# Layer 0's attention: one query ring for all head groups, a ring for weights alone with loads a unit sooner, late casts behind an exponential, modulation columns in another bank

## The chip, the cores and the metric

The kernel runs on one core of a Trainium2 chip. A core has five engines that each work through a queue of their own in order: PE (matrix products, into the accumulation memory PSUM), DVE and POOL (element-wise work), ACT (functions, copies and casts) and SP, which here only issues loads and stores. They meet through semaphores. The metric is the device time of one execution in microseconds (us).

## The reference, cut to what matters

Two layers of a backbone over 512 latent tokens and 256 context tokens of width 1024. Layer 0 mixes its tokens by two kinds of grouped attention, layer 1 by differential attention; each layer ends in a gated feed-forward block. The change touches only the mixer of layer 0 and, in it, the modulation vectors that are computed alongside:

```python
mx = (s_c @ mod_w[l] + mod_b[l])[:, None, :]          # modulation, six parts of 1024
hx = _rms(x, norm_mix_w[l]) * (1.0 + scx1) + shx1
qa, ka, va, qb, kb, vb = jnp.split(hx @ w_in, cuts, axis=-1)
qa, ka = _rope(_rms(qa, qn_a)), _rope(_rms(ka, kn_a))  # and the same for qb, kb
s = einsum(q, k) * scale; p = _softmax(s, sink)        # A: window of 128 and context; B: all tokens
out = einsum(p, v)                                     # then concatenated, @ w_out
```

There are 16 query heads of width 64. Four of them share a key and a value head; such a set of four is called a head group here. Groups 0 and 1 are of kind A, groups 2 and 3 of kind B. Products are made in single precision out of a rounded high part and a low part: a weight `wi` is cast on ACT to `wih` (the high part), and the rest `wil = wir - wih` is formed on DVE or POOL, so three products stand for one.

## The kernel before

**Tiles and steps.** The tokens are six tiles of 128 (four latent, two context). `in_proj0` projects one head group tile by tile: 24 products of 128x384 into one PSUM bank (`inps`), a copy to `qkv` on ACT (L529), norm and rotation on DVE and POOL, casts to `qd` and `kd`, and then two closures, `turn_q` and `turn_k`, which transpose the queries (`qpt`) and keys (`kpt`) on PE and copy them back on ACT (`qt`, L546, and `kT`, L553). `attend0` is a generator for one group and one tile: scores (`sc`), their maximum on DVE, the exponential on ACT (L601), the division on POOL (L613), transposes of the result (`ppt`, copied back by ACT at L626 and by DVE at L624) and the product with the values (`av`, copied by ACT at L634). The main loop takes 24 steps (b, t): in step (b, t) it attends group b, tile t, and puts the projection of one tile of group b+1 between the pieces.

**Order.** From the sixth step on PE's order is the order of the code (`manual_schedule`). Before that, and on all other engines throughout, the scheduler of the language sets the order when the program is built, by its own estimate of times.

**Weights.** A group needs four units of 256 rows of `ev_w_in`. `weights0` loads a unit with three DMAs into a staging tile `wir`, casts it on ACT (L507) and subtracts on DVE or POOL in turn (L508). The high and low parts go to rings of six tiles (`WBUF + 1`). Units 0 and 1 of group b+2 are made at step (b, 4), units 2 and 3 at the start of step (b+1, 0). The staging tiles come from `raw_tile`, a ring of two buffers (tag `raw`) that the modulation weights `modw` and the rotation table `rp` use as well.

**Modulation.** `mod_steps` computes 256 columns of one part: two loads of `modw`, 16 small products into the bank `acc0`, a copy `modr` (ACT, L185), and then, one step later, four products that turn the row into columns (`modcol`, L191), which DVE adds to `modc` (L279). `modcol` also stands in `acc0`, the bank of the projection's `inps`.

**Transposing banks.** `qpt`, `kpt` and `ppt` share two PSUM banks in turn (`tr0`, `tr1`); a transpose waits until the copy of what stood there before is done.

**Query tiles.** `qt` is a ring of six in a pool of the group's own: `odd` and `even` take turns, so there are two rings.

## Time and profile before

| what | value |
|---|---|
| median of 3 runs | 1686.17 us (1681.69 to 1688.62) |
| profiled execution | 1690.29 us, its span 1688.5 us |
| PE busy | 1629.1 us, 96% of the span |
| DVE, ACT, POOL busy | 1141.8, 935.7, 712.9 us |
| layer 0's attention with its projections | about 41 to 345 us of the span |

The span is the time from the first to the last instruction of the profiled execution; the rest up to its own time lies around it. In the rows below a time is a start in us from the span's beginning. A row of the timeline gives start, duration, engine, line of the code, operation, output and inputs, and, where the engine stood idle just before, how long and what ended it. In the rows of waits the numbers are the sum in us, how many, and the longest. `x4` at a row's end means that four instructions of one kind are merged in it.

### The profile page before, as it was taken

What the parts mean: (1) busy time and instruction counts of PE and PEld (TensorE: products, weight loads), DVE (VectorE), ACT (ScalarE), POOL (GpSimd) and SP (SyncE); (2) the same over time, 40 slices, a digit from 0 to 9 for tenths busy, and PEclk for the clock granted to TensorE, in tenths of its full rate; (3) what the DMA queues carried; (4) which work ended last, traced back from release to release, by engine and by line L of the source; (5) the groups of instructions that cost most, each with busy time, mean ns of one, the idle gap of its engine ahead of it and who ended that gap; (6) DMA issues with size and microseconds to landing.
All of it is one profiled execution on the core that took longest, in us unless ns stands there. A gap on an engine that the chain in (4) does not pass through costs nothing. (4 is left out here: it accounts for less than half of the span.)

```text
span 1688.5 us, 28522 instructions
## 1 busy us (share of the span) xinstructions
PE 1629.1 (96%) x10376; PEld 1466.7 (87%) x10376; DVE 1141.8 (68%) x1980; ACT 935.7 (55%) x2008; POOL 712.9 (42%) x872
## 2 busy tenths in 40 slices
PE   6999999899999999999999999999999999999998
PEld 3967787677999999998878799999987899999887
DVE  4765656554799988767767556666666598887433
ACT  5565555745456655545554456666666555555320
POOL 2665555621346554412413367776765342221000
PEclk8999999999999999999999999999999999999999
DMA  9222221411355555439866221111113333331431
GB/s 321 70 72 68 77 70 51 163 62 38 120 177 172 166 158 163 135 110 343 294 181 198 87 59 38 48 47 46 47 51 94 119 95 108 106 103 56 138 100 63
DMA packets 221693, 194.67 MB, mean 115 GB/s; under 512 B 20017, under 2 KB 206961, under 8 KB 221553
## 3 DMA queue, kind: packets, MB, share of 16 engines
q1 hardware_dynamic: 221200, 192.65, 37.1%
q8 instruction: 81, 1.33, 0.3%
q14 instruction: 60, 0.48, 0.1%
q10 hardware_dynamic: 352, 0.21, 0.0%
HBM read 179.94 MB, written 12.87 MB: 114 GB/s over the span
## 5 line engine op out<-in xcount | busy, mean ns | idle before, releaser
L928 ACT CAST wbh<-wr 128x512 fp32r<-128x512 f32 x170 | 104.8, 621 | 123.1 <-PE p L960 67.7
L960 PE MATMUL p<-hT,wbh 128*128 128x256 f32 (+1 forms) x752 | 154.0, 298 | 0.0
L474 PE MATMUL inps<-wih,hT 128*128 128x384 f32 x512 | 143.9, 343 | 2.6 <-ACT qkv L688 1.8
L938 POOL TENSOR_TENSOR wbl<-wr,wbh 128x512 fp32r<-128x512 f32 x43 | 58.5, 1360 | 173.5 <-ACT wbh L928 173.5
L960 PEld LDWEIGHTS p<-hT,wbh 128*128 128x128 f32 x752 | 122.1, 191 | 0.2
L938 DVE TENSOR_TENSOR wbl<-wr,wbh 128x512 fp32r<-128x512 f32 x127 | 107.1, 854 | 19.0 <-ACT wbh L928 14.9
L960 PE MATMUL p<-hT,wbl 128*128 128x256 f32 (+1 forms) x376 | 111.7, 297 | 0.0
L960 PE MATMUL p<-t,wbh 128*128 128x384 f32 (+1 forms) x480 | 110.8, 317 | 0.0
L613 POOL TENSOR_SCALAR Pt<-Pt,rc 128x256 f32<-128x256 f32 (+3 forms) x96 | 76.6, 810 | 67.0 <-DVE rc L610 58.2
L231 POOL TENSOR_TENSOR modp<-modp 128x512 f32<-128x512 f32 x40 | 56.5, 1412 | 113.5 <-ACT modp L230 113.5
L914 POOL TENSOR_TENSOR wr<-wr 128x512 f32<-128x512 f32 x40 | 62.3, 1558 | 92.5 <-DVE ws L919 92.5
L960 PE MATMUL p<-hTt,wbh 128*128 128x256 f32 (+1 forms) x480 | 100.8, 302 | 0.0
L474 PEld LDWEIGHTS inps<-wih,hT 128*128 128x128 f32 x512 | 93.4, 188 | 5.5 <-ACT qkv L688 2.8
L928 ACT CAST wbh<-ws 128x512 fp32r<-128x512 f32 x120 | 69.5, 580 | 44.4 <-PE p L960 29.7
L960 PE MATMUL p<-b,wbh 128*128 128x384 f32 x368 | 93.6, 335 | 0.5 <-DVE c L988 0.4
L224 DVE SCALAR_TENSOR_TENSOR ma<-modw,cols,ma 128x256 f32<-128x256 f32 x140 | 91.2, 651 | 2.5 <-DMA modw<-in_mod_w_dram 0.2
L601 ACT ACTIVATE Pt<-sc,nm 128x256 f32<-128x256 f32 (+3 forms) x96 | 67.8, 709 | 35.3 <-DVE nm L597 17.0
L474 PE MATMUL inps<-wil,hT 128*128 128x384 f32 x256 | 85.8, 335 | 0.0
L938 DVE TENSOR_TENSOR wbl<-ws,wbh 128x512 fp32r<-128x512 f32 x120 | 81.6, 680 | 1.7 <-ACT wbh L928 1.6
L960 PEld LDWEIGHTS p<-t,wbh 128*128 128x128 f32 x480 | 82.8, 189 | 0.0
L960 PEld LDWEIGHTS p<-hTt,wbh 128*128 128x128 f32 x480 | 78.4, 191 | 3.0 <-ACT modp L230 1.6
L474 PE MATMUL inps<-wihi,hT 128*128 128x384 f32 x256 | 75.7, 351 | 2.1 <-DVE modc L279 1.9
(359 smaller groups left out, 5214.0 us busy)
## 6 DMA issues: line engine op xcount, KB each, us to landing
modw<-in_mod_w_dram SPq DMA_DIRECT2D x96, 512.0 KB, 4.7
wr<-in_ffn_w_in_dram SPq DMA_DIRECT2D x176, 256.0 KB, 3.0
wdr<-in_ffn_w_out_dram SPq DMA_DIRECT2D x66, 512.0 KB, 3.7
wir<-in_od_w_in_dram SPq DMA_DIRECT2D x96, 128.0 KB, 2.3
hidm<-hid SPq DMA_DIRECT2D x44, 192.0 KB, 2.0
hr<-hidm SPq DMA_DIRECT2D x22, 192.0 KB, 3.5
x<-in_x_dram SPq DMA_DIRECT2D x8, 512.0 KB, 3.6
wir<-in_ev_w_in_dram SPq DMA_DIRECT2D x16, 256.0 KB, 3.6
```

Of the source, the lines that this page charges most:

```text
L224: nc.vector.scalar_tensor_tensor(acc, w[:, k], scale[k], acc, ALU.mult, ALU.add)
L231: nc.gpsimd.tensor_add(pr[:, 0:2], pr[:, 0:2], pr[:, 2:4])
L474: nc.tensor.matmul(ps, hs[j][:, k, :], ws[k // 2][z][:, k % 2, c0:c1], start=(k, j, z) == (0, 0, 0), stop=(k, j, z) == (KT - 1, 1, 0))
L601: turn["exp"] = nc.scalar.activation(p[:, :n], s, AF.Exp, bias=nm[:, c1], accum_out=sm[:, c1])
L613: nc.gpsimd.tensor_scalar(p[:, :n], p[:, :n], rc[:, hh:hh + 1], 1.0, ALU.mult, ALU.mult)
L914: nc.gpsimd.tensor_sub(w, raw[f, "G1"], w)
L928: nc.scalar.copy(hi, w)
L938: (nc.gpsimd if name == "G2" else nc.vector).tensor_sub(lo, raw[need[n]], f32(hi))
L960: nc.tensor.matmul(ps, w[:, k, :], H[b][h][:, k, :], start=first and k == 0 and q == 0, stop=final and k == 3 and q == 2, skip_group_check ...
```

## The change

There are six edits.

- `qt` is allocated in the pool of the whole attention (`at`), not in the group's own, so there is one ring of six for all groups.
- Staging tiles for the weights of groups 1 to 3 come from a ring of their own, two buffers with the tag `wir`; `raw` is left to `modw` and `rp`.
- In `weights0` the loads of unit 2 are issued when unit 1 is made and those of unit 3 with unit 2 (`loads`).
- The first loads of group 1 are put behind the load of `sink`.
- Units 2 and 3 of groups 2 and 3 are made after the first two pieces of step (b, 0), behind an exponential, and no longer ahead of that step.
- `modcol` in the attention stands in the bank `acc1`, that of `av`, and no longer in `acc0`.

```diff
-    def mod_steps(l, part, n, new_tile, pool, bank, wide=None, room=("modr", 1)):
+    def mod_steps(l, part, n, new_tile, pool, bank, wide=None, room=("modr", 1), cols_bank=None):
...
-        pc2 = p_1.tile([P, nb, 2], F32, name="modcol", tag=bank)
+        pc2 = p_1.tile([P, nb, 2], F32, name="modcol", tag=cols_bank or bank)
...
-    def weights0(b, wp, subs, new_tile=raw_tile, loads=((0, 1), (), (2,), (3,))):
+    def weights0(b, wp, subs, new_tile=raw_tile, loads=((0, 1), (2,), (3,), ())):
...
-                qt = st.tile([P, 4, P], F32R, name="qt", tag="qt", bufs=6)
+                qt = at.pool.tile([P, 4, P], F32R, name="qt", tag="qt", bufs=6)
...
-    nc.sync.dma_start(sink, dram_rows(ev_sink_a[0]))
+    turn["sink"] = nc.sync.dma_start(sink, dram_rows(ev_sink_a[0]))
...
-                mod_runs.append(mod_steps(*mods.pop(0), raw_tile, at.pool, "acc0"))
+                mod_runs.append(mod_steps(*mods.pop(0), raw_tile, at.pool, "acc0", cols_bank="acc1"))
...
-    units = weights0(1, wp.pool, (nc.gpsimd, nc.vector))
-    next(units)
+    def own_raw(shape, name):
+        return wp.pool.tile(shape, F32, name=name, tag="wir", bufs=2)
+
+    units = weights0(1, wp.pool, (nc.gpsimd, nc.vector), own_raw)
+    with behind("sink"):
+        next(units)
...
-                ws += units
+                if not b:
+                    ws += units
...
-                units = weights0(b + 2, wp.pool, (nc.gpsimd, nc.vector))
+                units = weights0(b + 2, wp.pool, (nc.gpsimd, nc.vector), own_raw)
...
                 transposes0(i - 1)
                 scores0(i)
+                if j == 0:
+                    with behind("exp"):
+                        ws += units
                 projected(n[0])
```

What the scheduler makes of it shows in the order of the instructions. On ACT, at the end of group 0's projection, just ahead of the first attention step, before:

```order
L449 ACTIVATE sq<-qkv 128x320 x2
L546 CAST qt<-qpt 128x512
L534 CAST qd<-qy 128x4x64
L553 CAST kT<-kpt 128x2x128
L538 CAST kd<-qy 128x128
L529 COPY qkv<-inps 128x384
L546 CAST qt<-qpt 128x512
```

and now:

```order
L449 ACTIVATE sq<-qkv 128x320
L507 CAST wihi<-wir 128x768 x2
L449 ACTIVATE sq<-qkv 128x320
L553 CAST kT<-kpt 128x2x128
L534 CAST qd<-qy 128x4x64
L538 CAST kd<-qy 128x128
L529 COPY qkv<-inps 128x384
L546 CAST qt<-qpt 128x512
```

The two casts are units 0 and 1 of group 2. They stood in the fourth step and now stand ahead of a key copy (`kT`) of group 0's last tiles.

On ACT, from the first attention step of group 1 into the next one, before:

```order
L626 COPY Pt<-ppt 128x4x128
L507 CAST wihi<-wir 128x768
L601 ACTIVATE Pt,sm<-sc,nm 128x256
L546 CAST qt<-qpt 128x512
L607 ACTIVATE es<-es 128x2
L507 CAST wihi<-wir 128x768
L626 COPY Pt<-ppt 128x4x128
L553 CAST kT<-kpt 128x2x128
L529 COPY qkv<-inps 128x384
```

and now:

```order
L546 CAST qt<-qpt 128x512
L601 ACTIVATE Pt,sm<-sc,nm 128x256
L507 CAST wihi<-wir 128x768 x2
L607 ACTIVATE es<-es 128x2
L626 COPY Pt<-ppt 128x4x128
L601 ACTIVATE Pt,sm<-sc,nm 128x256 x2
L607 ACTIVATE es<-es 128x2
L553 CAST kT<-kpt 128x2x128
L529 COPY qkv<-inps 128x384
L507 CAST wihi<-wir 128x768
L449 ACTIVATE sq<-qkv 128x320
L507 CAST wihi<-wir 128x768
```

The first pair of casts (units 2 and 3 of group 2) has moved behind the copy of the queries and an exponential. The second pair is units 0 and 1 of group 3, which stood four steps later; the copies of the step's values and transposes follow it.

On SP, the queue of the loads, the same part of the program, before:

```order
L177 DMA modw<-in_mod_w_dram 128x4x256 x2
L500 DMA wir<-in_ev_w_in_dram 128x2x256
L500 DMA wir<-in_ev_w_in_dram 128x2x64 x2
L500 DMA wir<-in_ev_w_in_dram 128x2x256
L500 DMA wir<-in_ev_w_in_dram 128x2x64 x2
L392 DMA rp<-in_rope_dram 128x512
L177 DMA modw<-in_mod_w_dram 128x4x256 x6
```

and now:

```order
L177 DMA modw<-in_mod_w_dram 128x4x256 x2
L392 DMA rp<-in_rope_dram 128x512
L177 DMA modw<-in_mod_w_dram 128x4x256 x2
L500 DMA wir<-in_ev_w_in_dram 128x2x256
L500 DMA wir<-in_ev_w_in_dram 128x2x64 x2
L500 DMA wir<-in_ev_w_in_dram 128x2x256
L500 DMA wir<-in_ev_w_in_dram 128x2x64 x2
```

Before, these loads of `wir` are units 2 and 3 of group 2; now those have been issued much earlier, and the ones shown are units 0 and 1 of group 3, ahead of which stands the table `rp`.

## Rows read from the trace of the kernel before

**Rows 1.** The page, busy time, share and instructions of PE:

```profile
PE 1629.1 (96%) x10376; PEld 1466.7 (87%) x10376; DVE 1141.8 (68%) x1980; ACT 935.7 (55%) x2008; POOL 712.9 (42%) x872
```

**Rows 2.** Windows: length, busy time of PE, PEld, DVE, ACT, POOL, PE's clock, DMA:

```profile
76.00:131.00 55.00, 49.87 (x363) 39.55 (x363) 35.63 (x109) 35.51 (x103) 37.06 (x64) 1.00 0.19 55
145.00:219.00 74.00, 68.85 (x521) 57.54 (x523) 47.31 (x127) 43.67 (x121) 39.83 (x66) 0.98 0.27 81
```

**Rows 3.** Waits of PE from 60 to 345 us:

```profile
PE ppt L621 <- ACT qt L546: 5.7, 5, 2.9
...
PE inps L474 <- DVE modc L279: 1.9, 3, 1.0
```

**Rows 4.** Timeline of PE, the stalls and one row without any:

```profile
74.38 0.55 PE L544 MATMUL qpt<-identr,qd 128*128 128x128 f32 x4 [0.63 <-ACT qt L546]
75.51 0.36 PE L552 MATMUL kpt<-identr,kd 128*128 128x128 f32 x2 [0.58 <-ACT kT L553]
...
149.88 0.66 PE L621 MATMUL ppt<-cst,Pt 128*128 128x128 f32 x4 [0.99 <-ACT qt L546]
...
156.96 1.22 PE L621 MATMUL ppt<-cst,Pt 128*128 128x128 f32 x6 [1.14 <-POOL Pt L613]
...
159.30 0.46 PE L544 MATMUL qpt<-identr,qd 128*128 128x128 f32 x4
...
198.24 0.66 PE L621 MATMUL ppt<-cst,Pt 128*128 128x128 f32 x4 [2.86 <-ACT qt L546]
...
225.77 1.10 PE L621 MATMUL ppt<-cst,Pt 128*128 128x128 f32 x8 [0.90 <-ACT qt L546]
```

**Rows 5.** Timeline of ACT, around 194 us:

```profile
193.53 0.84 ACT L507 CAST wihi<-wir 128x768 fp32r<-128x768 f32 x1 [0.86 <-DMA wir<-in_ev_w_in_dram]
...
196.09 0.83 ACT L507 CAST wihi<-wir 128x768 fp32r<-128x768 f32 x1 [1.22 <-issue]
...
197.61 0.57 ACT L546 CAST qt<-qpt 128x512 fp32r<-128x512 f32 x1
```

**Rows 6.** Timeline of SP's queue, two sets of loads of weights:

```profile
143.28 2.93 SPq L500 DMA_DIRECT2D wir<-in_ev_w_in_dram  x6
...
189.10 2.93 SPq L500 DMA_DIRECT2D wir<-in_ev_w_in_dram  x6
```

**Rows 7.** Windows around the longest stall, columns as in rows 2:

```profile
195.40:198.20 2.80, 0.00 (x0) 0.00 (x0) 2.10 (x2) 2.11 (x5) 1.61 (x3) 1.00 0.27 63
198.20:200.00 1.80, 1.76 (x13) 1.60 (x14) 1.19 (x4) 0.58 (x2) 0.13 (x1) 0.89 0.72 229
200.00:202.00 2.00, 2.00 (x9) 1.69 (x8) 1.50 (x4) 0.06 (x1) 1.45 (x2) 0.50 0.69 230
202.00:204.00 2.00, 2.00 (x11) 1.90 (x11) 0.00 (x0) 1.64 (x4) 0.20 (x1) 0.75 0.00 0
```

**Rows 8.** Timeline of ACT and DVE, around 70 us:

```profile
75.09 0.37 ACT L553 CAST kT<-kpt 128x256 fp32r<-128x256 f32 x1
...
68.06 0.99 DVE L508 TENSOR_TENSOR wilo<-wir,wihi 128x768 fp32r<-128x768 f32 x1
```

**Rows 9.** Timeline of ACT and POOL, 148 to 158 us:

```profile
148.05 0.84 ACT L507 CAST wihi<-wir 128x768 fp32r<-128x768 f32 x1 [1.23 <-issue]
...
153.33 0.48 ACT L529 COPY qkv<-inps 128x384 f32<-128x384 f32 x1 [0.74 <-PE inps L474]
...
157.78 0.59 ACT L626 COPY Pt<-ppt 128x512 f32<-128x512 f32 x1 [0.27 <-PE ppt L621]
...
148.96 1.82 POOL L508 TENSOR_TENSOR wilo<-wir,wihi 128x768 fp32r<-128x768 f32 x1 [1.43 <-ACT wihi L507]
```

**Rows 10.** DMA issues from 30 to 345 us: count, KB each, median us to landing:

```profile
wir<-in_ev_w_in_dram SPq DMA_DIRECT2D x16, 256.0 KB, 3.6
...
wir<-in_ev_w_in_dram SPq DMA_DIRECT2D x32, 64.0 KB, 3.2
```

## The prediction

> **What bounds the kernel now.** I read the busy times first: PE works for 96% of the span [rows 1], so the time is what PE computes plus what it stands idle, 59 us of 1688.5. The change computes nothing new (the same products, casts and loads); it can only move idle time and the clock. The second view is the windows by stage: layer 0's attention holds its share of that idle time, 55.00 - 49.87 = 5.13 us between 76 and 131, where the scheduler sets PE's order, and 74.00 - 68.85 = 5.15 us between 145 and 219, where the code does [rows 2]. The third view is PE's waits in 60 to 345 us: 5.7 us in five waits for the copy `qt` on ACT, and 1.9 us in three for `modc` on DVE [rows 3]. The fourth is the timeline, which says where those are: 0.99 at 149.88, 2.86 at 198.24, 0.90 at 225.77 [rows 4].
>
> The one at 198.24 is to be seen through ACT. The loads of two weight units are issued from 189.10 [rows 6]; ACT, which works in order, stands in front of the first cast until 193.53 and in front of the second until 196.09, and only then, at 197.61, comes the copy `qt` that frees the transposing bank that PE wants [rows 5]. The stall has a second price. PE did nothing for 2.80 us, and then the granted clock fell: 0.89, 0.50, 0.75 in the next three windows, that is to the lower of its two levels, 1.2 GHz, for about 3.4 us [rows 7]. Work lost: 0.11 x 1.8 + 0.50 x 2 + 0.25 x 2 = 1.70 us.
>
> **The change part by part.** All sums are against the profiled execution, 1690.29 us, its span 1688.5 and 1.8 around it. The median of the runs shown is 4.1 lower, and I subtract the sum from that median in the end.
>
> Casts at 198 and 225. In the new order the units of group 3 are cast elsewhere, so both waits go: -2.86 and -1.70 for the first, -0.90 for the second, together -5.5. What is late next there is PE itself, which has work in front of it.
>
> `modcol` in `acc1`. The projection no longer waits for DVE's addition, only for the copy `modr` that comes before it: -1.9. The new partner `av` is written a step later, and its own copy stands ahead of `modr` on ACT, so I cost the swap at nothing; if that cover failed, it would be the same three round trips, +1.9.
>
> One query ring. A query tile of group b+1 is turned two steps after the one whose place it takes was read, so the added wait is over before it begins: 0. What is queued behind it on ACT would be the step's copies.
>
> The ring for weights and the earlier loads. `modw` and `wir` no longer push each other out, but SP's queue is in order, and now the second pair of `modw` stands behind eight units of weights. PE asks for it only when the first modulation chunk is done, two attention steps after those units are cast, so 0.
>
> Now the two places at which the casts have come to stand. A unit's staging place is free when the unit two before it has been cast and subtracted; then come the load and the next cast. From the first issue of such a set to its first cast the rows show 193.53 - 189.10 = 4.4 and 148.05 - 143.28 = 4.8 us, to the second 196.09 - 189.10 = 7.0 [rows 5, 6, 9]. The landing times agree: 3.6 and 3.2 us for each of three loads that are issued half a us apart [rows 10].
>
> First place, ahead of the first attention step. Unit 3 of group 1 is subtracted at 68.06 to 69.05 [rows 8]; I allow 0 to 1.2 more, since the first loads of group 1 now wait for `sink`. Issue at 69.1 to 70.3; first cast 4.4 to 4.8 later; second cast 7.0 after the issue, at 76.1 to 77.3, and 0.84 long. Behind it on ACT stand a square and the key copy that PE's next transposes need, 0.37 each by the copy's row, so that copy ends at 77.7 to 78.9. Before it ended at 75.46 [rows 8], with PE right behind it at 75.51 [rows 4]. That is +2.2 to +3.4, and I take +2.8. PE would stand there in all for longer than the 2.80 us that cost it the clock, but broken by a few transposes; I take half of 1.70, +0.8. From below: if the loads come in time, the two waits of 0.63 and 0.58 might even go, -1.2. From above: 3.4 + 1.70 = +5.1.
>
> Second place, at the end of group 1's first step. Unit 2 of group 2 is subtracted on POOL by 150.78 [rows 9]; with one exponential and the copy `qt` (0.57, [rows 5]) now ahead of its cast I allow up to 1.4 more, so 150.8 to 152.2. Then the loads of group 3; the second cast ends 7.0 + 0.84 later, at 158.6 to 160.0. In the meantime ACT has nothing else to do from `qkv` (153.33) on, being in order. Behind the casts stand the copies `o` (taken as the key copy's 0.37) and `Pt` (0.59): done at 159.6 to 161.0, where before it was at 157.78 + 0.59 = 158.4. PE's next user of that bank is `qpt`, which began at 159.30 without any wait [rows 4]; it now begins 0.3 to 1.7 later, and I take +1.0. The 0.99 at 149.88 and the 1.14 at 156.96 [rows 4] vanish as such, but PE only arrives earlier at the new stall, so they aren't counted again. From below (loads in time): -0.99 - 1.14 = -2.1. From above: 1.7 and the clock's 1.70, +3.4.
>
> A rule of the Trainium skill speaks for and against this edit: "DMA: Bandwidth & Descriptors", section "Rules for kernel authors", says to issue a transfer early and to wait for it late. The loads are indeed issued earlier, but each cast now follows its issue in ACT's queue as closely as before, so by the rule nothing is hidden at these two places. The same page (section "Anatomy of one DMA") gives about 2.0 us fixed plus the bytes at 436 GB/s, for another way of issuing; an estimate by it for a unit of 393 KB is 2.9 us where the rows above show 4.4 to 4.8. By the page each of the two stalls would be some 1.6 us shorter and the sum below -6.0.
>
> The first five steps. The scheduler has re-dealt PE's rows between 76 and 131. Of the 5.13 us of idle time there about 1.7 are the `modc` waits; the other 3.5 are round trips to ACT, DVE and POOL. I take them as unchanged, 0, with -3.5 (all hidden) and +3.5 (twice as many) as ends.
>
> Sum: -5.5 - 1.9 + 2.8 + 0.8 + 1.0 = -2.8 us. By the profile 1687.5, against the median 1686.2 - 2.8 = 1683.4; I say 1683.
>
> **The rivals.** *All gains, no new stalls.* The loads land before ACT gets to the casts. For it: the casts are 0.84 long and ACT is busy for 55% of the span [rows 1]. Against it: every set of such loads in these rows was waited for. Sum -5.5 - 1.9 - 2.1 - 1.2 = -10.7, 1675.5.
>
> *The casts stop ACT for longer than the clock bears.* One mechanism at the two places: ACT stands in front of a load that could be issued only when a subtraction freed its place, and PE runs dry for over 2.8 us. For it: 7.0 us from issue to second cast and the clock in rows 7. Price: 5.1 and 3.4, and the round trips of the first five steps come late with it, +3.5: 12.0 less 7.4 of gains, +4.6, 1690.8. It decides from the point at which the two stalls cost more than the 7.4 us that go elsewhere. If the stall at 198 stays as well (4.6), +9.2, 1695.4.
>
> *The stall at 198 was not the casts'.* The second idle time of ACT there carries no named releaser [rows 5]; if something else holds, the 2.86 and 1.70 stay: -2.8 + 4.6 = +1.8, 1688.
>
> **How the numbers follow.** Forecast 0.60, no new stalls 0.13, clock 0.20 (of which 0.08 with the time beyond the bound), not the casts 0.07. A difference under 0.5%, 8.4 us, can't be told from none here; the three runs shown lie 6.9 us apart. Below 1677.7 lie most of the first rival and the lower edge of the forecast, 0.15; above 1694.6 the far part of the second, 0.08; between them 0.77. The forecast's own range is 1679 to 1688. The range of 8 in 10 reaches to the first rival below and past the second above: 1675.5 to 1691.5.
>
> **What would show it.** Right: no wait of PE for `qt` near 198 and 225, no clock below 0.9 there, none for `modc`; ACT idle in front of `wihi` near 73 and near 155, with PE waiting for `kT` near 76 and at `qpt` near 159. Wrong: casts at those two places without idle time before them (the time is lower), or PE's clock at 0.50 after them (higher), or waits of `mod` for its loads, which I hold for hidden.

## The result, and the profile after

| | before | after |
|---|---|---|
| median of 21 runs each | 1686.45 us (1680.78 to 1693.03) | 1689.27 us (1686.05 to 1692.62) |
| ratio, 95% interval | | 1.0017 [1.001, 1.0025] |
| profiled execution, its span | 1690.29, 1688.5 us | 1686.05, 1684.3 us |
| granted clock, mean | 0.994 | 0.998 |

The change made the kernel 2.8 us slower where 2.8 us faster was forecast. A warning ahead of all rows: the profiled execution of after is the shortest of its 21, and that of before is 3.8 above its own median. Executions of one program differ by several us, in good part because the clock falls at places where it holds in the next execution. So totals are compared by medians here, and places by the same products: every kernel that leaves the products alone records all 10376 of them, so a stretch can be taken from the start of one numbered product to another in each trace.

The page's row of PE in after, against [rows 1]:

```profile
PE 1624.5 (96%) x10376; PEld 1462.6 (87%) x10376; DVE 1141.9 (68%) x1980; ACT 935.4 (56%) x2008; POOL 711.0 (42%) x872
```

As many products; PE's busy time is 4.6 us less, and its mean granted clock 0.998 for 0.994. The waits of PE in after from 60 to 345 us, in the form of [rows 3]:

```profile
PE qpt L544 <- DVE Pt L624: 3.7, 2, 1.9
...
PE ppt L621 <- ACT qt L546: 2.4, 3, 1.0
...
PE qpt L544 <- DVE qd L535: 1.9, 1, 1.9
...
PE kpt L552 <- ACT kT L553: 1.2, 1, 1.2
PE inps L474 <- POOL wilo L508: 1.1, 1, 1.1
```

The waits for ACT's `qt` fell from 5.7 to 2.4 us and those for `modc` are gone, as forecast. In their place stand waits for DVE and POOL, which the forecast did not have. (`ppt`, `qpt` and `kpt` are the transposes, `inps` the projection.) Where they are, on PE's timeline of after, against [rows 4]:

```profile
69.91 0.51 PE L544 MATMUL qpt<-identr,qd 128*128 128x128 f32 x4 [1.93 <-DVE qd L535]
...
76.31 0.36 PE L552 MATMUL kpt<-identr,kd 128*128 128x128 f32 x2 [1.16 <-ACT kT L553]
...
149.02 0.54 PE L544 MATMUL qpt<-identr,qd 128*128 128x128 f32 x4 [1.78 <-DVE Pt L624]
...
153.31 0.44 PE L474 MATMUL inps<-wilo,hTc 128*128 128x384 f32 x1 [1.11 <-POOL wilo L508]
...
162.10 0.53 PE L544 MATMUL qpt<-identr,qd 128*128 128x128 f32 x4 [1.92 <-DVE Pt L624]
...
224.26 1.09 PE L621 MATMUL ppt<-cst,Pt 128*128 128x128 f32 x8 [0.97 <-ACT qt L546]
```

Around 198 us nothing is left of the stall and of the lower clock of [rows 7]. Windows of after (length, busy time of PE, PEld, DVE, ACT, POOL, PE's clock, DMA share, GB/s):

```profile
196.00:198.00 2.00, 2.00 (x16) 1.93 (x15) 0.90 (x3) 1.31 (x4) 0.83 (x2) 1.00 0.22 68
198.00:200.00 2.00, 2.00 (x19) 1.68 (x17) 1.49 (x4) 0.86 (x4) 1.15 (x2) 1.00 0.00 0
```

At 224.26 a wait of 0.97 us is left where 0.90 had been. ACT of after, just ahead of it:

```profile
222.17 1.55 ACT L507 CAST wihi<-wir 128x768 fp32r<-128x768 f32 x2
223.63 0.58 ACT L546 CAST qt<-qpt 128x512 fp32r<-128x512 f32 x1
```

These are units 2 and 3 of group 3, which edit 5 puts behind an exponential. They wait for no load any more, but they still stand in front of the copy `qt`.

The first of the two places to which the casts have moved, on ACT's timeline of after, against [rows 8]:

```profile
72.72 0.84 ACT L507 CAST wihi<-wir 128x768 fp32r<-128x768 f32 x1 [0.42 <-DMA wir<-in_ev_w_in_dram]
74.79 0.83 ACT L507 CAST wihi<-wir 128x768 fp32r<-128x768 f32 x1 [1.24 <-DMA wir<-in_ev_w_in_dram]
...
75.90 0.36 ACT L553 CAST kT<-kpt 128x256 fp32r<-128x256 f32 x1
```

This is the chain that was forecast (cast waits for its load, the key copy behind it, PE behind that), 1.4 to 2.6 us earlier: the copy ends at 76.26, not at 77.7 to 78.9. The clock stayed at 1.00. The wait of 1.93 us at 69.91, for the queries `qd` on DVE, stands ahead of these casts and was not forecast.

The second place, ACT of after, against [rows 9]:

```profile
157.81 0.83 ACT L507 CAST wihi<-wir 128x768 fp32r<-128x768 f32 x1 [1.58 <-DMA wir<-in_ev_w_in_dram]
...
158.92 0.82 ACT L507 CAST wihi<-wir 128x768 fp32r<-128x768 f32 x1
...
159.91 0.59 ACT L626 COPY Pt<-ppt 128x512 f32<-128x512 f32 x1
```

Here ACT keeps to the forecast: the second cast ends at 159.74 (forecast 158.6 to 160.0), the copy `Pt` at 160.50 (159.6 to 161.0). But that is not what PE waits for. The same stretch on DVE:

```profile
146.44 0.58 DVE L399 TENSOR_TENSOR rt<-rp,rw 128x256 f32<-128x256 f32 x1 [0.84 <-DMA rp<-in_rope_dram]
...
147.95 0.41 DVE L401 TENSOR_TENSOR rt<-rp,rw 128x256 f32<-128x256 f32 x1
148.28 0.68 DVE L624 COPY Pt<-ppt 128x512 f32<-128x512 f32 x1
...
160.50 0.94 DVE L508 TENSOR_TENSOR wilo<-wir,wihi 128x768 fp32r<-128x768 f32 x1
161.37 0.68 DVE L624 COPY Pt<-ppt 128x512 f32<-128x512 f32 x1
```

Twice a copy `Pt`, which frees the bank that `qpt` wants, stands behind other work on DVE: behind the four products of the rotation table (`rt`), and behind the subtraction that follows a late cast. The table got there through SP, whose queue in after reads, against [rows 6]:

```profile
143.54 0.34 SPq L392 DMA_DIRECT2D rp<-in_rope_dram  x1
...
153.29 2.93 SPq L500 DMA_DIRECT2D wir<-in_ev_w_in_dram  x6
```

With `wir` in a ring of its own, the load of `rp` no longer stands behind six loads of weights; it comes earlier, and so does what the scheduler puts behind it on DVE. In before the same four products ran at 153.53, after the step's `Pt` copy. From the issue of such a set of loads to the first cast the rows here show 157.81 - 153.29 = 4.5 us, to the second 5.6. "DMA: Bandwidth & Descriptors" of the Trainium skill ("Anatomy of one DMA") gave the forecast, for another way of issuing, an estimate of 2.9 us for a unit; the trace does not agree, and the rows decide.

All this is inside layer 0's attention. The following table goes over the whole program, from the first product to the last: time from one numbered product to another, minus the same in the profile of before. The three right-hand kernels and the second execution of before ("before 2") and of after ("after 2") come from the experiments below; (c) marks a stretch with a lower clock that before does not have there.

| stretch, us of before | before 2 | after | after 2 | edit 5 undone | edits 5, 6 undone | edit 6 alone |
|---|---|---|---|---|---|---|
| 0 to 131 | +0.6 | -0.1 | -0.1 | +0.4 | +0.6 (c) | +3.8 (c) |
| 131 to 160, second place | -1.0 | +3.0 | +3.1 | +3.2 (c) | +3.7 (c) | -0.8 |
| 160 to 192 | 0.0 | +0.1 | +1.2 (c) | 0.0 | 0.0 | 0.0 |
| 192 to 204, the old stall | -0.7 | -4.6 | -4.6 | -4.6 | -4.6 | -0.2 |
| 204 to 345 | -0.4 | +0.5 | +0.4 | -0.2 | -0.1 | -0.7 |
| 954 to 968, layer 1 | 0.0 | +1.8 | +1.8 (c) | 0.0 | +0.3 | +0.2 |
| 1099 to 1142, layer 1 | -0.2 | +1.4 | +1.9 | +1.4 | -0.1 | +1.4 |
| sum of these | -1.7 | +2.1 | +3.7 | +0.2 | -0.2 | +3.7 |
| all the rest, from 345 on | -3.8 | -6.2 | -3.0 | -5.8 | -4.9 | -5.4 |

The last row is why the sum of these stretches is not the difference of the two profiles. The profile of before has two falls of the clock in the rest, at 848 and 1261 us, each 3.4 us at 0.50 and so 1.7 us of work; what else differs there, in "before 2" as well, I have not traced. So a row says something of the change only where it goes beyond "before 2". Nor is the first row free of the clock: ahead of the attention the clock of before was at 0.50 from 32.3 to 42.6 us, that of after from 31.6 to 38.5. From 41 to 131 us alone the difference is +1.1 in after and 0.0 in "after 2".

The attention pays back at 131 to 160 most of what it gains at 192 to 204: up to 345 us after is 0.4 and "after 2" 1.5 us longer than "before 2". The rest of what the table shows against after, 3.2 and 3.7 us, stands 600 to 800 us behind the end of the changed attention. The first of the two places, on ACT and PE of after:

```profile
960.80 0.30 ACT L702 CAST kd<-qy 128x128 fp32r<-128x128 f32 x1 [2.98 <-POOL qy L691]
961.01 0.36 ACT L688 COPY qkv<-inps 128x256 f32<-128x256 f32 x1
...
961.62 1.49 ACT L358 ACTIVATE nhc<-npt,modc,aff 128x128 f32<-128x128 f32 x4
```

```profile
963.16 0.66 PE L352 MATMUL npt<-cst,nh 128*128 128x128 f32 x4 [1.62 <-ACT nhc L358]
```

The cast `kd` of layer 1 stands in front of the copy `qkv` and of the four activations `nhc`; in before it stands behind them. ACT waits 2.98 us for a product of POOL that is not in any hurry, and PE waits for `nhc`. No edit touches these lines: the scheduler dealt them anew, as I take it because its estimated times had shifted. In "after 2" ACT's order and its wait (2.99 us) are the same, but PE waits for nothing there: its clock fell at 958, behind a wait of 1.90 us that every profile here has, before's too, and 1.7 of the 1.8 us are that clock's. The second place is taken up with the experiments that explain it.

### The profile page after: what moved, and what is told of

Read it like the earlier page. It is cut to its first block, busy times and chain, and to the rows that moved or that the text cites. A ratio compares the mean times of both kernels' runs of the same rounds, so it can differ in the third digit from the quotient of the medians.

```text
span 1684.3 us, 28502 instructions
## 1 busy us (share of the span) xinstructions
PE 1624.5 (96%) x10376; PEld 1462.6 (87%) x10376; DVE 1141.9 (68%) x1980; ACT 935.4 (56%) x2008; POOL 711.0 (42%) x872
## 5 line engine op out<-in xcount | busy, mean ns | idle before, releaser
L230 ACT ACTIVATE modp<-modw,cols 128x256 f32<-128x256 f32 x160 | 68.3, 499 | 16.6 <-POOL ma L236 8.4
```

The lines of the kernel that those rows point to most:

```text
L230: nc.scalar.activation(pr[:, k], w[:, k], AF.Copy, scale=scale[k])
```

## The experiments

Ratios are against before on the same chip, with 95% intervals; diffs are against the kernel named.

**The two kernels once more.** No edit.

> The kernel before, unchanged. Theory A (fixed stalls): the kernel after loses its 2.8 us at three new stalls of PE in the first step of group 1 (1.78, 1.11 and 1.92 us in its profile, 4.8 in all, where before has 0.99 and 1.14), and gains too little at 198. Then the kernel before shows in a second profile the same waits: about 2.9 us at 198 for qt, followed by a granted clock of 0.5, and its executions lie at 1686 to 1687. Theory B (clock): the 2.8 us are executions in which the granted clock falls more often. Then the mean clock of these executions is above that of the kernel after (0.996 in the middle of 21), at 0.997 or more, and the profile of before with 0.994 was a bad draw: a new one is 2 to 4 us shorter. Either way the ratio to before is 1.000.

> The kernel after, unchanged. Its profiled execution took 1686.05 us at a mean clock of 0.998, the shortest of 21; the middle is 1689.3 at 0.996. Theory A: a second profile shows the same three stalls in the first step of group 1 (149, 153 and 162 us) with 4.8 us in all, and the rest of the difference to the first profile is chance. Theory B: it shows the granted clock at 0.5 in one or two places where the first profile had 1.00, of 3.4 us each; if they lie right behind the stalls of 149 to 162 us the stalls cause them, if they lie behind 345 us they have nothing to do with the change. Ratio to before 1.0017 in both.

Before: 1686.81 us, 1.0003 [0.9995, 1.0012]. After: 1690.06 us, 1.0025 [1.0015, 1.0034]. The stall at 198 and the clock behind it are in both profiles of before and in neither of after. In "after 2" the clock did fall behind the wait at the second place, which stands there too (1.72 us, at 162.24):

```profile
160.00:162.00 2.00, 0.52 (x3) 0.20 (x2) 1.97 (x4) 1.20 (x4) 1.88 (x3) 1.00 0.10 15
162.00:164.00 2.00, 1.76 (x9) 1.76 (x10) 0.67 (x3) 1.05 (x3) 1.87 (x3) 0.74 0.61 171
164.00:166.00 2.00, 2.00 (x9) 2.00 (x9) 0.97 (x3) 0.71 (x3) 0.63 (x3) 0.50 0.77 215
```

The same program, the same wait, and the clock falls in one execution and holds in the other. Over all timed runs the clock is not what makes after slower: its mean granted clock is 0.9953 in its 21 runs and 0.9943 in the 11 of the repeat, and 0.9943 in the 27 of before beside the repeat.

**Edit 5 undone (the units made ahead of step (b, 0), as before).** Against after:

```diff
-                if not b:
-                    ws += units
+                ws += units
...
-                if j == 0:
-                    with behind("exp"):
-                        ws += units
```

> The kernel after, but units 2 and 3 of groups 2 and 3 are made ahead of step (b, 0) again, not behind an exponential in it. Theory A: PE's wait for wilo at 153 (1.11 us) goes, because that low part is then ready before the second half of the projection asks for it; with the loads a unit sooner no new stall of ACT: 1 us less than the kernel after, ratio to before 1.001. Rival: the casts stand ahead of the step's exponentials and stop ACT there as they did before: no gain, ratio 1.0017 or more. Theory B: ratio 1.0017 with the mean clock of the kernel after.

1687.82 us, 1.001 [1.0001, 1.0019]: 1.5 to 2.2 below after. The 192 to 204 stretch keeps the whole gain of 4.6, so that gain isn't the late casts'. What the edit costs shows at three places of the table. At 204 to 345 it is 0.7 us: with the edit undone no cast stands ahead of the copy `qt` at 225, and PE does not wait there. At 954 to 968 it is 1.8: ACT's order in layer 1 is before's again, and the wait for `nhc` is gone. At 131 to 160 the waits at 153 (`wilo`) and 162 are gone, the one at 149 stays (1.98, now at 151.66), one of 1.07 at 144.49 is new, and so is a fall of the clock that costs 1.7; without the fall the stretch would be some 1.5 us shorter than in after (an estimate). How the price by runs divides between these is not shown.

**The casts of units 0 and 1 held back.** Against after:

```diff
-                    ws = [next(units) for _ in range(2)]
+                    with behind("exp"):
+                        ws = [next(units) for _ in range(2)]
```

> The kernel after, but the casts of units 0 and 1 of groups 2 and 3 are held behind an exponential of their own step (b, 4), so that the scheduler cannot place them four steps earlier. Theory A: the wait of PE for kT near 76 (1.16) and the one for DVE's copy Pt at 162 (1.92) go, the loads have long landed when the casts come, and near 198 no stall comes back: 3 us less than the kernel after, ratio to before 1.000 or a little below. Rival: the casts bring the stall at 198 back wherever they stand (2.9 and the clock's 1.7): 1.6 more than the kernel after, ratio 1.0025. Theory B: no change beyond 1 us in the fixed stalls; the time goes with the mean clock alone.

1693.88 us, 1.0041 [1.0029, 1.0054]: far from the 3 us less that were expected. The loads have long landed, so the casts wait for nothing, and still the place is dear: 5.2 us at 204 to 234, a fall of the clock included. ACT, DVE and PE:

```profile
200.34 1.57 ACT L507 CAST wihi<-wir 128x768 fp32r<-128x768 f32 x2
```

```profile
201.94 1.94 DVE L508 TENSOR_TENSOR wilo<-wir,wihi 128x768 fp32r<-128x768 f32 x1 [3.38 <-ACT wihi L507]
```

```profile
205.97 0.33 PE L621 MATMUL ppt<-cst,Pt 128*128 128x128 f32 x1 [1.43 <-POOL Pt L613]
```

The subtraction takes DVE for 1.94 us in the middle of a step's sums and divisions, and the step's `Pt` comes late. It isn't the wait for loads alone that costs; a unit's 0.8 us on ACT and 0.9 to 1.9 on DVE or POOL have to go somewhere.

**The rotation products held behind the `Pt` copy.** Against after, around the loop of the four `rt` products, with `turn["turned"]` set at the DVE copy `Pt`:

```diff
+        with behind("turned"):
             for j in range(2):
                 nc.vector.tensor_tensor(tb[:, j, :, 0, :], rp[:, :, 0, :], bc(w[:, j, :], 1, NTX), ALU.mult)
```

> The kernel after, with the four products rt of the rotation table held on DVE behind the copy Pt of the step, so that they do not stand ahead of the copy that PE waits for at 149.02 (1.78 us). PE's order is unchanged; the scheduler then also gives layer 1 the order of the kernel before. Theory A: 1.8 us less than the kernel after in the attention, ratio to before 1.0007. Theory L: the same in the attention and 1.6 in layer 1: 3.4 less, ratio 0.9997. Rival: the rt products, 1.8 us of DVE wherever they stand, stop the copies a microsecond later, and nothing is won in the attention.

1691.82 us, 1.0036 [1.0023, 1.0048]. The wait at 149 goes (131 to 147 is 2.0 us shorter than in after), so the `rt` products were its cause. But ACT and PE only come sooner to the casts:

```profile
156.85 0.83 ACT L508 CAST wihi<-wir 128x768 fp32r<-128x768 f32 x1 [2.89 <-DMA wir<-in_ev_w_in_dram]
```

```profile
158.58 0.51 PE L588 MATMUL sc<-kT,qt 128*128 128x256 f32 x2 [2.04 <-ACT Pt L602]
...
161.21 0.48 PE L622 MATMUL ppt<-cst,Pt 128*128 128x128 f32 x1 [1.90 <-POOL Pt L614]
```

Granted clock from 162 to 166: 0.50. 147 to 160 is 5.6 us longer than in before. This is like the prediction's second rival: ACT stands in front of a load, PE runs dry, the clock falls, at one of its two places. In after's profile that did not happen.

**Layer 1's `kd` held back.** Against after, first behind `qkv` of the next tile, then behind `nhc` (with `turn["nhc"]` set at the activation):

```diff
-                late.append((0, first.finish(t, banks[t], 0 < t < NTX)))
+                late.append((0, first.finish(t, banks[t], 0 < t < NTX or t == CTX_FIRST[0])))
...
+            if t == CTX_FIRST[0]:
+                kept = waiting.pop()
...
+        with behind("nhc"):
+            kept()
```

The first two of these lines alone:

> The kernel after, with one edit in layer 1, 620 us behind the change: the cast kd of the first tile is held behind the copy qkv of the next one. That gives ACT, DVE and POOL there the order that they have in the kernel before (in the kernel after the scheduler has moved kd ahead of qkv, ACT stands 2.98 us for it at 960.80, and PE 1.62 us at 963.16). Theory L (layer 1): this stall is a good half of the measured 2.8 us. Then it goes: 1.6 to 1.8 us less than the kernel after, ratio to before 1.001, and no wait of PE for nhc on ACT near 960. Theory A (attention: the three new stalls of 149 to 162 us are the cause): no change, ratio 1.002.

1688.47 us, 1.0016 [1.0007, 1.0025]. The expectation was wrong in one thing: this does not bring before's order back, since `kd` then stands behind `qkv` but still ahead of `nhc`. All of them:

> The kernel after, with the cast kd of the first tile in layer 1 held behind the four activations nhc that follow the next tile's copy qkv and square. (The earlier hold put it behind qkv alone, still ahead of the square and of nhc; without a fall of the clock such an order showed 1.4 us of waiting for nhc, with one none but the clock's loss.) Theory L: now the whole 1.5 to 1.9 us near 963 goes, and no fall of the clock is needed to hide it: 1.7 less than the kernel after, about 1687.6, ratio to before 1.001. Rival: kd, now some 3 us later, is late for the transposes kpt at about 985: the time comes back there, ratio 1.002.

1688.06 us, 1.0021 [1.0011, 1.0032]; no wait for `nhc`, 0.0 at 962 to 968. But the time does not follow the profile: 1.0016 and 1.0021 are not clearly below after's 1.0017 and 1.0025. These runs were on another chip than the repeats; against before on their own chip their medians are 2.9 and 2.5 us longer, after's two are 2.8 and 3.7. So the price of 1.8 us is read from a profile, and no run that undoes this order alone shows it. A possible reason is in the traces: in three of the six profiles with `kd` behind `nhc` the clock falls near 958 all the same, behind the wait of 1.90, and 954 to 968 is 1.5 us longer than in before.

**Two products more, in before.** Does any disturbance upstream do this? Before with two extra products of 128x2 in one modulation chunk at about 310 us, alone and with each hold:

```diff
-        for b in range(nb):
+        for b in (0,) * 2 * ((l, part, n) == (0, 4, 3)) + tuple(range(nb)):
```

> The kernel before, with two more products of 128x128 by 128x2 in one modulation chunk at about 320 us (one column is computed three times; the output is the same). Nothing else is edited, and the attention's order stays that of the kernel before, but the scheduler then gives ACT, DVE and POOL in layer 1 the order of the kernel after (kd ahead of qkv), and PE's program is four instructions longer from there on (that of the kernel after is three longer). Theory L: the stall at about 963 appears (1.6 to 1.8 us) and so do the three small ones that the kernel after has at 1101, 1109 and 1138 (0.7, 0.3 and 0.8): 1.7 to 3.5 us slower than before, ratio 1.001 to 1.002, with nothing of the change in it. Theory A: 0.2 us for the two products, ratio 1.000.

> The kernel before with the two more products, and with kd held behind qkv in layer 1 as in the kernel before. Theory L says of the small waits at 1101 and 1138 that a load of weights is passed on the DMA engines by a 16 KB piece of PE's program, whose place is set by how many instructions PE has run; then these stay (PE's program is four longer): 0.6 to 1.8 us slower than before, ratio 1.0003 to 1.001. If they hang on the order of ACT and DVE in layer 1 they go with it: ratio 1.000. Theory A: ratio 1.000.

> The kernel before with two more small products at about 310 us and kd held behind nhc in layer 1. Theory L: of what the two products cost without this hold (ratio 1.0025) the stall near 963 goes, the loads that meet PE's program at 1097 and 1136 stay (0.8 to 1.4 us): 1687 to 1688, ratio 1.001. If the ratio stays above 1.002, the order in layer 1 was not the price.

1690.18 us, 1.0025 [1.0013, 1.0037]; with the hold behind `qkv` 1688.65, 1.0021 [1.001, 1.0031]; with the hold behind `nhc` 1692.68, 1.0047 [1.0034, 1.006]. The two products gave layer 1 after's order of `kd`, with before's attention: the order out there hangs on shifts that small. As a price of that order the three runs are no good. By the expectation of the last one, a ratio above 1.002 means that the order was not the price, and it is 1.0047 with the order restored. But that kernel also loses 4.5 us at 305 to 345, with two falls of the clock; the one held behind `qkv` loses 3.1 there, with one fall, and the unheld one 1.3 with none. So they speak neither for 1.8 us nor clearly against it.

**Edit 6 alone, on before.** `modcol` in `acc1`, nothing else:

> The kernel before with one edit of the six alone: the columns modcol in the bank acc1. The prediction's term: PE's three waits for modc (1.9 us) go, and nothing takes their place: 1.9 less, 1684.2, ratio 0.999. Rival: the waits go but PE meets the next round trips to ACT and DVE of the same steps earlier by as much, since those set the pace in 76 to 131 us: ratio 1.000, with the stretch 42 to 131 us as long as before. Layer 1 keeps the order of the kernel before; if PE's program is longer by a few instructions, the 1.3 us of the loads at 1097 and 1136 come on top: ratio 1.0007.

1689.2 us, 1.0025 [1.0014, 1.0036], by medians 3.6 us longer than before on the same chip. Forecast for this edit: -1.9. The `modc` waits do go, but another comes. ACT and PE of this kernel, and the windows:

```profile
108.68 0.83 ACT L507 CAST wihi<-wir 128x768 fp32r<-128x768 f32 x1 [1.63 <-DMA wir<-in_ev_w_in_dram]
109.42 0.37 ACT L185 COPY modr<-mod 128x256 f32<-128x256 f32 x1
```

```profile
109.84 0.58 PE L474 MATMUL inps<-wihi,hT 128*128 128x384 f32 x1 [1.85 <-ACT modr L185]
```

```profile
108.00:110.00 2.00, 0.16 (x1) 0.16 (x2) 1.54 (x4) 1.32 (x3) 1.69 (x4) 1.00 0.27 80
110.00:112.00 2.00, 2.00 (x7) 2.00 (x8) 0.97 (x4) 1.44 (x5) 0.83 (x2) 0.50 0.61 202
```

`mod` itself still stands in `acc0`, so the projection still waits for the copy `modr`, and in this order that copy stands behind a cast that waits for its load. Besides, 1099 to 1142 in layer 1 is 1.4 us longer.

**Edits 5 and 6 undone, `kd` held.** What is left of the change is the query ring, the ring `wir`, the earlier loads and the load behind `sink`:

```diff
-                mod_runs.append(mod_steps(*mods.pop(0), raw_tile, at.pool, "acc0", cols_bank="acc1"))
+                mod_runs.append(mod_steps(*mods.pop(0), raw_tile, at.pool, "acc0"))
```

> After with edit 5 and edit 6 undone (casts ahead of step (b, 0), modcol in acc0 as before), and layer 1's kd kept behind nhc; what is left of the change is the one query ring, the ring wir, the earlier loads and the load behind sink. Theory (edit 6 is worth nothing: what modc gives, modr takes): within 1 us of the run with edit 5 undone alone, 1687 to 1688.5. Rival by the prediction (modcol in acc1 is worth 1.9): 1689.5 or more. Rival by the run of edit 6 alone on before (+2.8): 1685.

1685.07 us, 0.999 [0.9981, 1.0]. The third of the expected ways came out. Against edit 5 undone (which has before's order of `kd` without a hold) the difference is edit 6, but for the hold: it costs 1687.82 - 1685.07 = 2.75 us in the changed kernel, and 3.6 by medians in the old one. The `modc` waits don't come back with `modcol` in `acc0` (0.2 us in one wait from 60 to 345): it was the new order that took them away. Half of the 2.75 is at 1099 to 1142, and this pair of kernels shows how. The DMAs of after while one load of layer 1's weights is under way, then of this kernel (a queue's packets, MB and share of the 16 engines; below it the loads issued in that window, KB each, us to landing):

```profile
q8 instruction: 1, 0.02, 3.5%
...
wir<-in_od_w_in_dram SPq DMA_DIRECT2D x1, 128.0 KB, 3.3
```

```profile
q1 hardware_dynamic: 814, 0.39, 75.9%
...
wir<-in_od_w_in_dram SPq DMA_DIRECT2D x2, 128.0 KB, 2.2
```

In after a packet of 16 KB from the instruction queue (PE's program, by the count below) travels on one of the DMA engines while the load does, and the load lands after 3.3 us instead of 2.2. Then ACT's cast, and PE, first in after, then here:

```profile
1134.82 0.83 ACT L379 CAST wih<-wir 128x768 fp32r<-128x768 f32 x1 [1.44 <-DMA wir<-in_od_w_in_dram]
```

```profile
1137.61 0.39 PE L474 MATMUL inps<-wil,hTc 128*128 128x256 f32 x1 [0.96 <-POOL wil L380]
```

```profile
1133.35 0.84 ACT L379 CAST wih<-wir 128x768 fp32r<-128x768 f32 x1 [0.32 <-DMA wir<-in_od_w_in_dram]
```

```profile
1136.57 0.39 PE L474 MATMUL inps<-wil,hTc 128*128 128x256 f32 x1 [0.27 <-POOL wil L380]
```

Counted from one numbered product ahead of it, the packet starts at 8.9 and 8.6 us in the two profiles of before and 8.85 here, just behind the load's landing at 8.6, but at 7.4 in after, 7.2 with edit 5 undone and 7.4 with edit 6 alone. "Runtime: NRT & Kernel Launch" of the Trainium skill ("Instruction fetch mechanics") says that an engine fetches its program in blocks of 16 KiB, 256 instructions each, by a DMA queue of its own, at a cost that is mostly hidden. The trace agrees on the blocks (81 such packets; 81 x 256 is within 16 of PE's 2 x 10376 products and weight loads). From a load that it meets it is not hidden here. Why edit 6 moves the block by 1.5 us of products I have not settled. The other half of the 2.75 isn't pinned down: 42 to 131 is 1.6 us shorter than with edit 5 undone, but that stretch also depends on how the first 40 us went.

**Sixteen products more, in before, with `kd` held behind `qkv`.** The two products of above made sixteen, to move the packet on purpose.

> The kernel before with sixteen more small products in one modulation chunk at about 310 us (with two in the run before), and kd held behind qkv in layer 1. All other orders are those of the run with two. If a 16 KB piece of PE's program that passes on the DMA engines is what delays the loads of weights at 1097 and 1136, its place moves again, by some ten to sixteen products to the front: it then comes before the loads at 1136 and PE's wait there (0.8 us more than in the kernel before) is gone, while the one at 1097 may hit the load before. If the small waits come from the order of DVE or ACT, they stay as in the run with two: 0.1, 0.3 and 0.8 us at 1101, 1109 and 1138. The products themselves cost about 1 us at 310 us; ratio to before 1.001 to 1.002 in both, so it is read from the trace.

1693.45 us, 1.004 [1.0027, 1.0052], with a fall of the clock near 315 us as above. For the packet it answers: it starts at 4.4 us, ahead of this load, the cast comes at 9.0 as in before, and 1108 to 1142 shows 0.0 for +1.0 in after; but it now meets the load before, and 1099 to 1105 shows +0.6 (after: +0.4).

**The units spread over the steps.** Against after, units 0 and 1 of groups 2 and 3 made one each in steps (b, 2) and (b, 3) behind the exponential, the `rt` products a step later, `kd` held behind `qkv`; then the same with edit 5 undone; then with `kd` behind `nhc`:

```diff
-                if j == 4 and b < 2:
-                    ws = [next(units) for _ in range(2)]
+                if j in (2, 3) and b < 2:
+                    with behind("exp"):
+                        nws.append(next(units))
```

> The kernel after, with four edits together: units 0 and 1 of groups 2 and 3 are made in steps (b, 2) and (b, 3), one in each, behind an exponential (not two in step (b, 4), placed by the scheduler as early as (b, 0)); their loads are issued in step (b, 2); the products rt of the rotation table stand a step later, behind the copy Pt; and in layer 1 the cast kd is held behind the copy qkv. Theory L: the stalls of 149 and 162 go (3.7 us of the kernel after) and the one at 963 (1.6), the small ones at 1101 and 1138 stay (1.4): 1684, ratio to before 0.999; without a stall near 198 the kernel is at last faster than before. Rival (casts themselves, as in the run with held casts): each unit costs DVE 1 and POOL 1.8 us in front of what PE waits for, wherever it stands, and two stalls of 1 to 2 us come in steps (b, 2) and (b, 3): 1687 to 1688, ratio 1.001.

> The same four edits, and units 2 and 3 of groups 2 and 3 are made ahead of step (b, 0) as in the kernel before, not behind an exponential in it. Theory L: PE's wait for wilo at 153 (1.1 us) goes too: 1683, ratio 0.998. Rival: as there, the casts of those units stop ACT in the last step of the group before (PE waited 1.07 us for the copy Pt at 144.49 in the run with only this edit), nothing is won against the other run: 1684 or 1687.

> The run with spread casts and units 2 and 3 made ahead of step (b, 0) (ratio 1.0015), with kd held behind nhc in layer 1. Its attention showed 4.6 us won near 198 and 4.2 lost again between 160 and 192, where the casts now stand. Theory L: 1.5 us near 963 go: 1687.3, ratio 1.0006; faster than before only if the loads near 1097 and 1136 miss PE's program. Rival as for the other run: kd late for kpt, ratio 1.0015.

1689.74 us, 1.0023 [1.0013, 1.0032]; 1688.83, 1.0015 [1.0004, 1.0026]; 1689.44, 1.002 [1.001, 1.0031]. No gain, where the theory had 1684, 1683 and 1687.3: 131 to 160 comes out below before (-1.7 to -2.4), and the same work then costs 4.2 to 4.7 us at 160 to 192. At neither of the other places were the casts free: 4.2 to 4.7 us here, 5.2 held back. The last of the three shows 0.0 at 954 to 968 where the second shows +1.6, but its time is no shorter: a second pair in which `kd` held behind `nhc` brings nothing that the runs can tell.

**Edit 5 undone, `rt` behind the `Pt` copy, `kd` behind `nhc`.** The best of the pieces together; `rt` in the same step, then a step later:

> After with edit 5 undone (units 2 and 3 of groups 2 and 3 made ahead of step (b, 0), as before), the four products of the rotation table held behind the copy Pt that DVE makes in the step, and layer 1's kd kept behind nhc. Theory (the rt products ahead of DVE's Pt copy hold the queries at the second place, the moved kd holds layer 1): the wait of qpt at about 151.7, 1.98 us with edit 5 undone, goes; no wait for nhc near 963. By the run with edit 5 undone (1687.8) less 2.0: about 1686, ratio 0.999 to 1.000, about 3 us under after, no clear difference from before. Rival (the work on DVE or ACT costs PE wherever it stands): the wait comes back in the next step, 1688 to 1690.

> The same, but the four rt products are made in the next step, behind its copy Pt on DVE. Theory: as the run beside it, 1685 to 1687, since DVE has more room there. Rival: the rotation of the next group's first queries now waits for rt, PE waits for qd or kd a step later, 1688 to 1690.

1687.93 us, 1.0012 [1.0003, 1.0021], and 1686.93, 1.0005 [0.9995, 1.0014]. The first missed 1686: its `qpt` wait for the `Pt` copy is gone, but PE waits elsewhere in the same steps, as the rival had it:

```profile
147.33 0.65 PE L633 MATMUL av<-Pt,vv 128*64 128x256 f32 x4 [1.79 <-ACT Pt L627]
...
162.22 1.22 PE L622 MATMUL ppt<-cst,Pt 128*128 128x128 f32 x6 [1.85 <-POOL Pt L614]
```

The second came within its forecast, 1685 to 1687, and can't be told from before. No kernel run here beats before by more than the measurement can tell; the nearest is edits 5 and 6 undone, 0.1% below. Edits 1 to 4 were not timed apart from each other.

## Why the prediction was wrong, point by point

- **Casts at 198, -2.86 and -1.70.** Right in size (-4.6 for -4.56, in both profiles of after; against "before 2", whose stall was shorter, -3.9) and in cause, the place of casts that wait for loads. But it belongs to edits 1 to 4, among them the ring `wir` and the earlier loads: it stays with edit 5 undone and is absent with edit 6 alone.
- **The wait at 225, -0.90.** Wrong: it is there after the change, 0.97 us. The two casts were taken to be elsewhere, but edit 5 puts units 2 and 3 of group 3 (1.55 us on ACT) in front of the copy `qt` there; with edit 5 undone the wait is gone.
- **`modcol` in `acc1`, -1.9.** The step that failed by most, as far as runs show, and wrong in sign: the edit costs 2.75 us in the changed kernel and 3.6 in the old one. The argument took one of the two things in `acc0` that the projection waits for, counted its wait as pure gain, and held the rest of the program still. In the old kernel a wait of 1.85 for the other one (`modr`) came in its place, with a fall of the clock; in the changed one about 1.5 us are at 1099 to 1142, in layer 1, and the rest is not pinned down.
- **One query ring, the ring for weights, 0.** No wait for either in the rows. But the forecast checked what the ring pushes back (`modw`), not what it lets forward: `rp`, and with it `rt` ahead of DVE's `Pt` copy.
- **First place, +2.8 and +0.8 for the clock.** The wait is there, 1.2 us for `kT` behind a cast, with one of 1.9 for `qd` before it; no clock fell. In "after 2" they are 0.7 and 1.2. With the first five steps and the `modc` waits in the same stretch the net from 41 to 131 us is +1.1 and 0.0 in the two profiles, where the forecast had +2.8 + 0.8 - 1.9 = +1.7.
- **Second place, +1.0.** Too small, by a mechanism that was missed: +3.0 and +3.1. ACT did what was forecast; PE waited for DVE and POOL, which have the other half of the unit (`wilo`) and the `rt` products. Of the 3.0 us 2.4 are at 131 to 147, ahead of the second pair of late casts, and 2.0 of them go when the `rt` products are held.
- **The rest of the program, not a term at all.** The other step that failed. The sum went from 60 to 345 us and took the other 1340 as unchanged because no edit touches them. The scheduler deals the whole program anew, and the order of layer 1 shows the moved `kd` without any run. The profiles show 1.8 us there, and 1.4 to 1.9 at 1099 to 1142, where a block of PE's program fell on a load (traced at 1136, 0.7 us of it in after). How much of the 1.8 an average execution pays stays open, since neither pair of runs with `kd` held showed it.

By runs alone the account is this: edits 1 to 4 -0.8 us (1685.07 against 1685.86, not clear of none), edit 6 +2.75, edit 5 +1.5 to +2.2, together +3.4 to +4.2; the medians of after say +2.8 and, in the repeat, +3.7. The table's sums, +2.1 and +3.7, are of the same size, but they leave out the rest, which differs by more from profile to profile. Two rivals come close in time, and by luck: the second (1690.8), though in after's profile no clock fell at either place and in "after 2" it fell behind a wait of 1.72 us, not one of 2.80, and the third (1688), though the stall at 198 did go.

## What to carry to other kernels

Where a scheduler sets the order, a change reaches as far as the program: compare the order of every engine to the very end, and look for a price of each row that moved, before summing what the edit itself does. A load let forward takes its consumers with it on an engine that works in order, so ask of every ring that is split what now comes sooner, not only what comes later. And time the edits apart: here one gain of 4.6 us stood beside two edits that did not belong to it and that the runs price at 2.75 and at 1.5 to 2.2 us of loss. A stall that goes in a profile is not yet time that goes in the runs: time that too.

## What the runs showed of the hardware that I had not expected

- A 16 KB block of PE's own program on the DMA engines makes a load that it meets land 1.1 us later (3.3 for 2.2 us), and PE wait 0.96 us (1.17 in "after 2") where it waited 0.27. Moved ahead of that load, it leaves it alone and meets the one before. Where it falls changes with edits far upstream.
- The same wait, in the same program, is followed by a fall of PE's clock in one execution and not in the next (162 us: 1.00 and 0.50). One profile on each side can mislead by more than the change is worth: here it showed after 4.2 us faster.
